# A two-layer hybrid decoder trunk: block products from the fourth inner tile on, weight rests and summed inputs formed by transfers

## The chip, the cores and the metric

The kernel runs on one core of a Trainium2 chip. The metric is the device time of one execution in microseconds (us); the median of several runs is compared. One further execution is taken under the hardware profiler, and all views quoted here are of that one.

The engines are named as the profile names them: PE is the matrix engine (PEld its weight loads), DVE the vector engine, ACT the scalar engine, POOL the GpSimd engine, SP the engine that issues most transfers. Work on one engine runs in the order in which it was laid down when the program was built; engines wait for one another by semaphores.

## The reference

A sequence of 512 tokens of width 1024 passes two layers. The first mixes tokens with a state-space layer (S5), the second with forgetting attention (FoX); behind each stands a gated feed-forward network with a causal convolution of width 3. Every sub-layer's input is normed and modulated.

```python
def modulate(x, g, shift, scale):
    return rmsnorm(x, g) * (1.0 + scale) + shift

def conv_ffn(h, w_up, conv_w, conv_b, w_down):
    up = h @ w_up                        # 1024 -> 2 * 2816
    a, b = jnp.split(up, 2, axis=-1)
    ap = jnp.pad(a, ((0, 0), (CONV_W - 1, 0), (0, 0)))
    a_conv = conv_b
    for i in range(CONV_W):
        a_conv = a_conv + ap[:, i:i + S] * conv_w[i]
    return (jax.nn.silu(a_conv) * b) @ w_down

for i in range(DEPTH):                   # DEPTH = 2
    hn = modulate(h, norm_g[i, 0], *...)
    m = s5_mixer(hn, ...) if i % 2 == 0 else fox_mixer(hn, ...)
    h = h + gate * m
    hn = modulate(h, norm_g[i, 1], *...)
    h = h + gate * conv_ffn(hn, ...)
return rmsnorm(h, final_g)
```

All inputs are float32.

## The kernel before

**Products in parts.** A float32 operand is kept as two parts, hi (the value rounded to the matrix engine's float32r type) and lo (the rest, value minus hi). A product of two operands is three matmuls into one accumulator: hi with hi, hi with lo, lo with hi (`mms`, L304). Weights come in by a transfer issued on SP into a buffer "raw" (`raw`, L192; three buffers). `put_parts` makes hi on ACT (L287) and lo on DVE, `lo = raw - hi` (L288). hi and lo of weights lie in five buffers each (w_hi and w_lo), used in turn; a buffer comes free when PE has used it.

**A network.** Each network's inner width of 2816 is 22 inner tiles f of 128. An inner tile has two weight tiles of 1024 x 128: 2f for the convolved branch, 2f+1 for the other. `gated` takes their products: convolution in three steps (ACT L618, DVE L620 twice), SiLU on ACT (L623), the product with the other branch on DVE (L627), and the split of the result into ghi and glo (ACT L287, DVE L288). The inner tiles come in four groups of 6, 5, 6 and 5. While a group is made, `down` multiplies the group before it with w_down (eight products in all per group, dealt out over the group's tiles) and adds them to the residual stream h (DVE L378). In the first network `tick` adds two rows of later modulation parameters per tile from f=6 on (DVE L256).

**Whole tiles and block tiles.** A whole tile (`up`) is 96 matmuls of 128 x 256: two weight tiles, 8 slices of the input width, 2 halves of the tokens, 3 parts. A block tile (`quarters`) takes the two weight tiles as a 2 x 2 matrix of blocks a11, a12, a21, a22 (each four slices deep) and the input as 2 x 2 blocks (first and second half of its width, first and second half of the tokens), and forms the result from seven block products in place of eight: 7 x 4 x 3 = 84 matmuls (L566). For that it sums blocks of weights on DVE (L537: s1 to s4, in the buffers "sums", four instructions 512 wide), splits them (two more splits 1024 wide, one 512 wide for a22), copies four partial results on ACT (L573), and adds partial results on DVE (L537, four instructions 256 wide, out of the accumulators).

Its input forms t1 to t4 are made once per network by `forms_x`: first the normed input's two parts are added, x = a_hi + a_lo, into two buffers of 128 x 4 x 512 (DVE L500, four instructions), then four forms are subtracted (DVE L506) and split (ACT L287, DVE L288). `forms_x` is a generator; the network's loop takes three steps of it in each whole tile from f=1 on, and what is left before the first block tile.

`WHOLE_TILES` (L49) names the whole tiles of each network: f = 0, 1, 2, 3, 4, 8, 11, 14, 17, 20 in the first, f = 0 to 3 in the second. So there are 12 and 18 block tiles. f=0 and f=1 begin as one group of three weight tiles (the head), first half of the tokens first, so that the second half of the input can still be normed meanwhile (DVE L445 and L449, ACT L448).

**Order.** The framework's scheduler lays every engine's instructions in one order when the program is built, from the order in which they are written, from their dependences, and from its estimate of when each becomes ready. So a change in one place can move instructions on several engines. In the S5 layer the last step of `s5_inputs` (a product, then transposes by PE, L979, L988 and L990, copied out by ACT L989) stands among the first products of the next stage; its accumulators are taken from the pool "aux" (four), while large products mostly use the pool "mmp" (four).

Of the kernel before, what the change touches and what calls it, by code (L numbers as in the profile page):

```python
# [8 lines left out]
F32 = mybir.dt.float32  # L9
# [3 lines left out]
ALU = mybir.AluOpType  # L13
# [32 lines left out]
ROWS_FROM = 0  # L46
GROUPS = (6, 5, 6, 5)
TAIL = 4
WHOLE_TILES = (0, 1, 2, 3, 4, 8, 11, 14, 17, 20), (0, 1, 2, 3)  # L49
SUMS = (0,) * 6 + (2,) * 16  # L50
FIRST = (("c", (KT,)), ("s5_prm", (3, G // 2)))
REST = (
# [11 lines left out]
class Trunk:  # L64
# [6 lines left out]
    def __init__(self, tc, io, ctx):  # L71
        self.tc, self.nc, self.io, self.ctx = tc, tc.nc, io, ctx
        nc = self.nc
        pool = lambda name, bufs, **k: ctx.enter_context(tc.tile_pool(name=name, bufs=bufs, **k))
        self.const = pool("const", 1)
        self.act = pool("act", 1)
        self.wpool = pool("wpool", 3)
        self.tmp = pool("tmp", 2)
        self.small = pool("small", 2)
        self.dram = pool("dram", 1, space=DRAM)  # L80
        self.mm = pool("mm", 4, space=PSUM)
        self.aux = pool("aux", 4, space=PSUM)
        self.bg, self.late = [], ()
        self.acc = None
        self.pending = None
        self.rests, self.odd = 0, False
# [185 lines left out]
    def split(self, src, shape, pool=None, bufs=WB, off=None):  # L272

        if off:
            more = TAIL_ROOM - math.prod(shape[1:])
            hi, lo = (self.wide(pool, n, {"bufs": bufs}, F32R, more, off[n], shape) for n in ("w_hi", "w_lo"))
        elif pool:
            hi, lo = (pool.tile(shape, F32R, name=n, bufs=bufs) for n in ("w_hi", "w_lo"))
        else:
            hi = self.wpool.tile(shape, F32R, name="w_hi", bufs=WB)  # L280
            lo = self.rest(shape, odd=self.odd)
        self.put_parts(hi, lo, self.raw(shape, src))
        return hi, lo

    def put_parts(self, hi, lo, src):
        nc = self.nc
        nc.scalar.activation(hi, src, AF.Copy)  # L287
        self.late = (nc.vector.tensor_tensor(lo, src, hi.bitcast(F32), ALU.subtract).ins,)  # L288

    def weights(self, w, nk, *pool):  # L290
# [199 lines left out]
    def forms_x(self, pool, x, b):  # L490
# [1 line left out]
        nc = self.nc  # L492
        H, N = KT // 2, S // 2
        t1, t2 = HALVES
        normed = self.last_lo.ins
        for j, t in enumerate(b):
            for c in HALVES:
                k = slice(j * H, (j + 1) * H)
                with self.tc.issue_after(normed):
                    nc.vector.tensor_tensor(t[:, :, c], x[0][:, k, c].bitcast(F32), x[1][:, k, c].bitcast(F32), ALU.add)  # L500
                yield
        self.tx = {}

        def form(n, u, v):
# [21 lines left out]
        form(3, b[1][:, :, t2], b[0][:, :, t2])  # L526
        yield

    def quarters(self, pool, l, f, x, finish):

        nc = self.nc
        H, N = KT // 2, S // 2
# [4 lines left out]
        sub = lambda o, u, v, op=ALU.subtract: nc.vector.tensor_tensor(o, u, v, op)  # L537
        w = {}

        def parts(src, names, where=None):  # L540
            shape = [P, len(names) * H, P]
            hi, lo = where or (self.wpool.tile(shape, F32R, name="w_hi", bufs=WB), self.rest(shape, odd=True))
            self.put_parts(hi, lo, src)
            for j, n in enumerate(names):
                w[n] = hi[:, j * H:(j + 1) * H], lo[:, j * H:(j + 1) * H]

        parts(a, ("a11", "a12"))
        sub(c[:, 0], a21, a22, ALU.add)
        sub(c[:, 1], c[:, 0], a11)
        parts(c.rearrange("p n k m -> p (n k) m"), ("s1", "s2"))  # L550
# [43 lines left out]
        sub(ob[:, t1], p1, c4)  # L594
        finish(2 * f + 1, ob, slice(0, S))

    def ffn(self, i, l, x, nxt, whole, sums=()):

        nc, tc = self.nc, self.tc
        with tc.tile_pool(name=f"ffn{l}", bufs=1, reuse_waits="tile") as pool:  # L600
# [49 lines left out]
            for q, n in enumerate(GROUPS):  # L650
                for j, f in enumerate(range(first[q], first[q + 1])):
# [14 lines left out]
                    else:  # L666
                        while todo:
                            if next(todo[0], True):
                                todo.pop()
                        self.quarters(pool, l, f, x, gated)  # L670
                    if q:
                        down(q - 1, range(j * KT // n, (j + 1) * KT // n))
                    self.tick(sums[f] if f < len(sums) else 0)
            self.done()
            down(last, range(KT), tail=TAIL, tail_pool=(pool, 4, TAIL_OFF))
# [122 lines left out]
class S5(Trunk):  # L798
# [163 lines left out]
    def s5_inputs(self, m):  # L962
# [10 lines left out]
        dd = pool.tile([P, P], F32, name="dd", bufs=1)  # L973
        nc.sync.dma_start(dd, self.io["s5_dd"][m])
        part = lambda k, r: x[:, k, r].rearrange("p c j -> p (c j)")
        pk = self.aux.tile([P, 2, P], F32, name="aux")
        for r in range(2):
            for k in range(H4):
                nc.tensor.matmul(  # L979
# [298 lines left out]
class Kernel(S5):  # L1278
# [32 lines left out]
    def fox_values(self, pool, x):  # L1311
# [9 lines left out]
        def load(q):  # L1321
# [3 lines left out]
            out = []  # L1325
            for a in range(0, KT, step):
                j = min(step, KT - a)
                hi, lo = self.split(src[:, a:a + j, :], [P, j, n])
                out += [(hi[:, i, :], lo[:, i, :]) for i in range(j)]
            return out  # L1330

# [172 lines left out]
def build(tc, io, out, stop=None):  # L1504
    with ExitStack() as ctx:
# [97 lines left out]
```

## Time and profile before

| | us |
|---|---|
| median of 3 runs | 1193.88 |
| the runs | 1202.24, 1192.06, 1193.88 |
| the profiled execution | 1197.65 |
| its span, first to last instruction | 1195.9 |
| PE busy | 1174.1 |
| DVE busy | 988.7 |
| ACT busy | 592.4 |
| POOL busy | 62.6 |

The span runs from the first to the last instruction of the profiled execution; 1.75 us of its time lie outside. In the timeline views each row gives the start, the length, the engine, the source line, the operation, the tile written and the tiles read, shapes, and how many instructions were merged, with the idle time before it and what ended that in brackets. The views by stretch give the start and end of a stretch, its length, and for PE, PEld, DVE, ACT and POOL the busy time and the count of instructions, then the granted clock of PE, the busy share of the transfer engines and GB/s. Where a stretch is asked for one source line, only the engines that run it are listed. Lengths of instructions that follow each other overlap a little, so what one costs in a row of them is read from start to start.

### The profile page before, as it was taken

Reading aid. Unit: us, or ns where it says so; the run is one execution under the profiler, and the core shown is the slowest. Engines: PE = TensorE matmul, PEld = TensorE weight load, DVE = VectorE, ACT = ScalarE, POOL = GpSimd, SP = SyncE. Lnnn points to the kernel's source line nnn. Section 1 sums busy time; section 2 is a strip of 40 time slices with the busy share of each in tenths; the row PEclk is TensorE's granted clock in tenths of the full one; section 3 lists DMA queues with packets and bytes.
Section 4 is the critical chain, followed back from the end, with each engine's and each line's share of the span. In section 5 each row is a group of like instructions: output and inputs, shape, how many; then the busy total and the mean of one; then the engine's idle time right before and its main releaser. Section 6 shows DMA issues by size and latency. Waiting matters only on the chain.

```text
span 1195.9 us, 21116 instructions
## 1 busy us (share of the span) xinstructions
PE 1174.1 (98%) x8243; PEld 1026.5 (86%) x8243; DVE 988.7 (83%) x1824; ACT 592.4 (50%) x1069; POOL 62.6 (5%) x114
## 2 busy tenths in 40 slices
PE   7999999999999999999999999999999999999997
PEld 2455687899999999999899788878999999999987
DVE  8899977889888888887776788866899888888855
ACT  2554525346544454453453566554466555555543
POOL 1000000000000000000000443330000000000000
PEclk9999989999999999999999999999999999999999
DMA  9687758822264455554514655523123342343331
GB/s 359 226 256 251 230 167 303 295 92 89 87 204 131 159 174 170 185 184 139 194 36 138 209 185 166 200 76 97 47 75 96 124 124 86 111 124 95 104 88 72
DMA packets 73234, 183.83 MB, mean 154 GB/s; under 512 B 23231, under 2 KB 25503, under 8 KB 72111
## 3 DMA queue, kind: packets, MB, share of 16 engines
q1 hardware_dynamic: 72847, 181.96, 46.6%
q8 instruction: 65, 1.06, 0.4%
q10 hardware_dynamic: 288, 0.52, 0.1%
q14 instruction: 34, 0.28, 0.1%
HBM read 175.53 MB, written 6.92 MB: 153 GB/s over the span
## 4 chain that ended last, share of the span: by engine, by line
PE 86%; DVE 7%; DMA 3%; ACT 2%; issue 1%; POOL 0%; SPq 0%; DVEq 0%; ACTq 0%; POOLq 0%
PE mmp L304 42%; PE mmp L566 15%; PE aux L566 6%; PE mmp L1167 4%; PE mmp L1344 3%; PE mmp L1197 2%; DVE w_lo L288 2%; PE aux L1490 2%; PE aux L1473 1%; PE aux L1061 1%; PE aux L1053 1%; PE mmp L221 1%; PE aux L1443 1%; ACT w_hi L287 1%; DMA raw<-in_w_down 1%
## 5 line engine op out<-in xcount | busy, mean ns | idle before, releaser
L287 ACT ACTIVATE w_hi<-raw 128x1024 fp32r<-128x1024 f32 (+4 forms) x197 | 176.0, 900 | 146.9 <-PE mmp L304 75.5
L288 DVE TENSOR_TENSOR w_lo<-raw,w_hi 128x1024 fp32r<-128x1024 f32 (+4 forms) x197 | 203.4, 1036 | 29.7 <-ACT w_hi L287 25.2
L304 PE MATMUL mmp<-a_hi,w_hi 128*128 128x256 f32 (+1 forms) x600 | 185.9, 311 | 0.0
L304 PE MATMUL mmp<-a_hi,w_lo 128*128 128x256 f32 (+1 forms) x600 | 182.8, 306 | 0.0
L304 PE MATMUL mmp<-a_lo,w_hi 128*128 128x256 f32 (+1 forms) x600 | 182.7, 305 | 0.0
L304 PE MATMUL mmp<-ghi,w_hi 128*128 128x512 f32 (+1 forms) x392 | 143.9, 367 | 0.0
L304 PE MATMUL mmp<-glo,w_hi 128*128 128x512 f32 (+1 forms) x392 | 143.9, 367 | 0.0
L304 PE MATMUL mmp<-ghi,w_lo 128*128 128x512 f32 (+1 forms) x392 | 143.6, 366 | 0.0
L304 PEld LDWEIGHTS mmp<-a_hi,w_hi 128*128 128x128 f32 x600 | 112.4, 188 | 7.6 <-issue 2.6
L304 PEld LDWEIGHTS mmp<-a_hi,w_lo 128*128 128x128 f32 x600 | 112.5, 188 | 6.4
L304 PEld LDWEIGHTS mmp<-a_lo,w_hi 128*128 128x128 f32 x600 | 112.6, 188 | 4.8
L287 ACT ACTIVATE w_hi<-sums 128x1024 fp32r<-128x1024 f32 x68 | 71.6, 1060 | 65.9 <-DVE sums L537 27.4
L566 PE MATMUL mmp<-w_hi 128*128 128x256 f32 x360 | 99.6, 277 | 0.0
L566 PE MATMUL mmp<-w_hi,w_lo 128*128 128x256 f32 x360 | 99.5, 276 | 0.0
L566 PE MATMUL mmp<-w_lo,w_hi 128*128 128x256 f32 x360 | 99.4, 276 | 0.0
L288 DVE TENSOR_TENSOR w_lo<-sums,w_hi 128x1024 fp32r<-128x1024 f32 x68 | 82.4, 1220 | 7.6 <-ACT w_hi L287 6.5
L256 DVE CUSTOM_DVE_ANT_0 ada_raw<-ada_raw,ada_c,rest 128x1024 f32<-128x1024 f32 x64 | 83.7, 1326 | 5.1 <-DMA ada_raw<-in_ada_rows 5.1
L304 PEld LDWEIGHTS mmp<-ghi,w_lo 128*128 128x128 f32 x392 | 73.6, 188 | 12.3
L304 PEld LDWEIGHTS mmp<-ghi,w_hi 128*128 128x128 f32 x392 | 73.6, 188 | 11.2
L304 PEld LDWEIGHTS mmp<-glo,w_hi 128*128 128x128 f32 x392 | 73.6, 188 | 11.1
L378 DVE SCALAR_TENSOR_TENSOR h<-mmp,par,h 128x512 f32<-128x512 f32 (+1 forms) x98 | 62.9, 649 | 23.4 <-PE mmp L304 23.3
L566 PEld LDWEIGHTS mmp<-w_hi 128*128 128x128 f32 x360 | 67.6, 188 | 0.1
(317 smaller groups left out, 2833.0 us busy)
## 6 DMA issues: line engine op xcount, KB each, us to landing
raw<-in_w_up SPq DMA_DIRECT2D x88, 512.0 KB, 3.4
ada_raw<-in_ada_rows SPq DMA_DIRECT2D x64, 512.0 KB, 4.2
raw<-in_ada_w SPq DMA_DIRECT2D x32, 512.0 KB, 5.5
raw<-in_w_down SPq DMA_DIRECT2D x32, 384.0 KB, 3.2
raw<-in_w_down SPq DMA_DIRECT2D x32, 320.0 KB, 3.1
nf<-nfd SPq DMA_DIRECT2D x8, 1152.0 KB, 5.7
raw<-in_fox_qk SPq DMA_DIRECT2D x16, 512.0 KB, 3.2
h<-in_x SPq DMA_DIRECT2D x8, 512.0 KB, 5.5
```

What stands on the lines that cost most here:

```text
L221: self.last_mm = nc.tensor.matmul(ps[32 * qq:32 * qq + 32, :], self.sc32[:, k, :], w[:, q * S:(q + 1) * S], start=(step is steps[0]), stop ...
L256: nc.vector.tensor_tensor_reduce(w, w, self.crow, 1.0, self.ada_b[:, i, m:m + 1], ALU.mult, ALU.add, self.par[i][:, m:m + 1])
L287: nc.scalar.activation(hi, src, AF.Copy)
L288: self.late = (nc.vector.tensor_tensor(lo, src, hi.bitcast(F32), ALU.subtract).ins,)
L304: self.last_mm = self.nc.tensor.matmul(o, wt, xt[:, cols], start=(k == 0 and n == 0), stop=(k == nk - 1 and n == 2),)
L378: self.nc.vector.scalar_tensor_tensor(h, v, self.par[i][:, 16 + m:17 + m], h, op0=ALU.mult, op1=ALU.add,).ins,
L566: self.last_mm = nc.tensor.matmul(o, wt[:, k], xt[:, k], start=(first and k == 0 and n == 0), stop=(k == H - 1 and n == 2), skip_group_che ...
L1053: nc.tensor.matmul(yp[g2][:, k, :], t[:, 2 * k + g2], u[:, g, :], start=(k == 0), stop=False, skip_group_check=True,)
L1167: nc.tensor.matmul(ps, w[m][:, k, :], x[:, k], start=(k == 0), stop=(k == KT - 1))
L1197: nc.tensor.matmul(gps[m], wt, xt[:, k], start=(k == 0 and part == 0 and xt is yhi), stop=(k == KT - 1 and part == 1))
L1344: self.last_mm = nc.tensor.matmul(ps[q, b][:, :n], xt[:, k, tb], wt, start=(k == 0 and i == 0), stop=(k == KT - 1 and i == 2),)
L1490: nc.tensor.matmul(pv[:, c * P:], self.v[:, hp, k, r].rearrange("p t d -> p (t d)"), pp[:, r, c + 3 * k:NB + 3 * k, :].rearrange("p b t -> ...
```

## The change

Four edits. The whole tiles are now f = 0, 1, 2 in both networks, so each has 19 block tiles. The adds of the input's parts become twelve transfers per network issued by POOL: four copies of a_hi (512 KB) and eight transfers of a_lo (256 KB) that add to what lies in the buffer. In the first network, lo of each block tile's first weight tile and of the down weights of all but the last group is made as minus hi on ACT, to which a transfer issued by POOL adds the weights once more from DRAM; the same holds for two loads of the attention's value weights. And the last step of `s5_inputs` takes its first accumulator from the other pool.

```diff
-WHOLE_TILES = (0, 1, 2, 3, 4, 8, 11, 14, 17, 20), (0, 1, 2, 3)
+WHOLE_TILES = (0, 1, 2), (0, 1, 2)
...
-        self.put_parts(hi, lo, self.raw(shape, src))
+        self.put_parts(hi, lo, self.raw(shape, src), src if self.by_dma else None)
         return hi, lo
 
-    def put_parts(self, hi, lo, src):
+    def put_parts(self, hi, lo, src, again=None):
         nc = self.nc
         nc.scalar.activation(hi, src, AF.Copy)
+        if again is not None:
+            nc.scalar.activation(lo, hi.bitcast(F32), AF.Copy, scale=-1.0)
+            nc.gpsimd.dma_start(lo, again, accum_op=ALU.add)
+            return
         self.late = (nc.vector.tensor_tensor(lo, src, hi.bitcast(F32), ALU.subtract).ins,)
...
     def forms_x(self, pool, x, b):
...
-        normed = self.last_lo.ins
-        for j, t in enumerate(b):
+        for n, step in enumerate((4, 2)):
             for c in HALVES:
-                k = slice(j * H, (j + 1) * H)
-                with self.tc.issue_after(normed):
-                    nc.vector.tensor_tensor(t[:, :, c], x[0][:, k, c].bitcast(F32), x[1][:, k, c].bitcast(F32), ALU.add)
-                yield
+                for j, t in enumerate(b):
+                    for a in range(0, H, step):
+                        k = slice(j * H + a, j * H + a + step)
+                        nc.gpsimd.dma_start(
+                            t[:, a:a + step, c], x[n][:, k, c].bitcast(F32), accum_op=ALU.add if n else ALU.bypass
+                        )
...
-    def quarters(self, pool, l, f, x, finish):
+    def quarters(self, pool, l, f, x, finish, by_dma):
...
-        parts(a, ("a11", "a12"))
+        parts(a, ("a11", "a12"), again=self.io["w_up"][l][2 * f] if by_dma else None)
...
-                        self.quarters(pool, l, f, x, gated)
+                        self.quarters(pool, l, f, x, gated, by_dma)
                     if q:
+                        self.by_dma = by_dma
                         down(q - 1, range(j * KT // n, (j + 1) * KT // n))
+                        self.by_dma = False
...
-        pk = self.aux.tile([P, 2, P], F32, name="aux")
+        pk = self.mm.tile([P, S], F32, name="mmp")[:, :2 * P] if m == KT - 1 else self.aux.tile([P, 2 * P], F32, name="aux")
+        pk = pk.rearrange("p (n c) -> p n c", n=2)
...
+                self.by_dma = q == 1
                 hi, lo = self.split(src[:, a:a + j, :], [P, j, n])
+                self.by_dma = False
...
-        x = k.ffn(1, 0, x, k.norm_mod(2), WHOLE_TILES[0], SUMS)
+        x = k.ffn(1, 0, x, k.norm_mod(2), WHOLE_TILES[0], SUMS, True)
```

In the changed kernel L287 and L292 are the two halves of a split, L289 and L290 the pass that makes minus hi and the transfer that adds, L504 the transfers of the input's sum, L511 the forms, L542 the sums, L571 the block products, L625 the convolution's steps and L632 the gate product.

More of the change, by code (lines that the diff above doesn't have):

```diff
@@ L85, in __init__ @@
         self.pending = None
-        self.rests, self.odd = 0, False
+        self.rests, self.odd, self.by_dma = 0, False, False
         self.ones = self.const.tile([P, P], F32, name="ones")
@@ L538, in quarters, with parts @@
         w = {}
-        def parts(src, names, where=None):
+        def parts(src, names, where=None, again=None):
             shape = [P, len(names) * H, P]
             hi, lo = where or (self.wpool.tile(shape, F32R, name="w_hi", bufs=WB), self.rest(shape, odd=True))
-            self.put_parts(hi, lo, src)
+            self.put_parts(hi, lo, src, again)
             for j, n in enumerate(names):
                 w[n] = hi[:, j * H:(j + 1) * H], lo[:, j * H:(j + 1) * H]
-        parts(a, ("a11", "a12"))
+        parts(a, ("a11", "a12"), again=self.io["w_up"][l][2 * f] if by_dma else None)
         sub(c[:, 0], a21, a22, ALU.add)
@@ L595, in quarters, with ffn @@
         finish(2 * f + 1, ob, slice(0, S))
-    def ffn(self, i, l, x, nxt, whole, sums=()):
+    def ffn(self, i, l, x, nxt, whole, sums=(), by_dma=False):
         nc, tc = self.nc, self.tc
```

## The prediction

> **What bounds the kernel now.** I read the page first (busy time, chain of waits), then busy time by stage, then the timelines of VectorE (DVE) and ScalarE (ACT) around the first block tile of each network.
>
> ```profile
> PE 1174.1 (98%) x8243; PEld 1026.5 (86%) x8243; DVE 988.7 (83%) x1824; ACT 592.4 (50%) x1069; POOL 62.6 (5%) x114
> PE 86%; DVE 7%; DMA 3%; ACT 2%; issue 1%; POOL 0%; SPq 0%; DVEq 0%; ACTq 0%; POOLq 0%
> ```
>
> TensorE (PE) is busy nearly always and holds 86% of the chain that ended last. The next view gives busy time in stretches: a whole tile (f=8), a block tile (f=5), two down products and a middle stretch of the first network, then the first three block tiles of the second.
>
> ```profile
> core 0: us, PE busy (x) PEld busy (x) DVE busy (x) ACT busy (x) POOL busy (x), PEclk, DMA share, GB/s
> 310.34:319.89 9.55, 9.55 (x87) 9.55 (x86) 8.03 (x13) 6.62 (x11) 0.00 (x0) 1.00 0.28 88
> 351.20:362.11 10.91, 10.91 (x97) 10.91 (x96) 7.29 (x10) 3.40 (x4) 0.00 (x0) 1.00 0.54 182
> 450.00:480.00 30.00, 30.00 (x236) 28.80 (x235) 26.22 (x41) 15.03 (x23) 0.00 (x0) 1.00 0.56 177
> 890.93:919.82 28.89, 28.89 (x255) 28.79 (x253) 28.53 (x44) 18.12 (x31) 0.00 (x0) 1.00 0.35 117
> ```
>
> A whole tile holds PE for 10.91 us, a block tile for 9.55, or 0.1137 per matmul, 1.36 per product of twelve. PE never idles there. But in the second network DVE is busy 28.53 of 28.89 us: PE and DVE are level, and three tiles take 0.24 more than 3 x 9.55. So matmuls taken away pay only while DVE's splits, sums and forms keep ahead.
>
> **The change, part by part.** *Matmuls.* Seven tiles of the first network and one of the second become block tiles: 8 x 1.36 = **-10.9**, the whole of what can be won in the networks.
>
> *The forms come early.* The first block tile is now f=3. In the first network it starts two whole tiles before 310.34, at 288.5, in the second one before 890.93, at 880.0. DVE's prices are read from start to start in its timeline, first network:
>
> ```profile
> 270.19 4.62 DVE L500 TENSOR_TENSOR x<-a_hi,a_lo 128x1024 f32<-128x1024 f32 x4
> 274.73 2.71 DVE L620 SCALAR_TENSOR_TENSOR conv<-mmp,conv_wb,conv 128x511 f32<-128x511 f32 x4
> 277.36 2.35 DVE L288 TENSOR_TENSOR w_lo<-raw,w_hi 128x1024 fp32r<-128x1024 f32 x2
> 279.63 1.27 DVE L627 TENSOR_TENSOR conv<-conv,mmp 128x512 f32<-128x512 f32 x2
> 280.82 1.22 DVE L288 TENSOR_TENSOR w_lo<-raw,w_hi 128x1024 fp32r<-128x1024 f32 x1
> 281.96 1.28 DVE L288 TENSOR_TENSOR glo<-conv,ghi 128x512 fp32r<-128x512 f32 x2
> 283.17 1.22 DVE L506 TENSOR_TENSOR sums<-x 128x1024 f32<-128x1024 f32 x1
> 284.30 0.74 DVE L620 SCALAR_TENSOR_TENSOR conv<-mmp,conv_wb,conv 128x511 f32<-128x511 f32 x1
> ...
> 299.48 1.28 DVE L537 TENSOR_TENSOR sums<-raw 128x512 f32<-128x512 f32 x2
> 300.69 0.68 DVE L627 TENSOR_TENSOR conv<-conv,mmp 128x512 f32<-128x512 f32 x1
> ...
> 331.08 0.42 DVE L537 TENSOR_TENSOR nm_t<-mmp,nm_h 128x256 f32<-128x256 f32 x1
> 331.42 0.74 DVE L620 SCALAR_TENSOR_TENSOR conv<-nm_t,conv_wb,conv 128x510 f32<-128x510 f32 x1
> ```
>
> Four conv steps take 2.63, a wide split 1.14, a form 1.13, a gate product, a gate rest or a weight sum 0.60, one conv step 0.66 (a quarter of the four), an output sum 0.34.
>
> The first place is DVE's order at the entry of the first network (x_2514 and x_2515 are the two summed halves of the input, sums the forms). Before:
>
> ```order
> L500 TENSOR_TENSOR x_2514<-a_hi,a_lo 128x4x256 x2
> L500 TENSOR_TENSOR x_2515<-a_hi,a_lo 128x4x256 x2
> L620 SCALAR_TENSOR_TENSOR conv<-mmp,conv_wb,conv 128x511 x2
> L620 SCALAR_TENSOR_TENSOR conv<-mmp,conv_wb,conv 128x510 x2
> L288 TENSOR_TENSOR w_lo<-raw,w_hi 128x1024 x2
> ```
>
> and now:
>
> ```order
> L625 SCALAR_TENSOR_TENSOR conv<-mmp,conv_wb,conv 128x511 x2
> L625 SCALAR_TENSOR_TENSOR conv<-mmp,conv_wb,conv 128x510 x2
> L511 TENSOR_TENSOR sums<-x_2514 128x1024
> L511 TENSOR_TENSOR sums<-x_2515,sums 128x1024
> L632 TENSOR_TENSOR conv<-conv,mmp 128x512 x2
> ```
>
> The adds are gone, the forms stand right behind the conv steps. The conv steps wait for the head's products, so DVE gains no time ahead of them: 274.73 stays. From there to the split of s1, which f=3 needs, now stand 4 conv steps (2.63), 4 forms (4.52), their 4 splits (4.54), 3 gate products and 3 rests (3.6), 2 conv steps (1.32), 4 weight sums (2.42), an output sum (0.34) and the split (1.14): 20.5, so 295.2. PE puts three products ahead of s1, to 292.6: **+2.5**. If DVE or PE shift a little, 0 to 4.
>
> Second network:
>
> ```profile
> 861.71 4.63 DVE L500 TENSOR_TENSOR x<-a_hi,a_lo 128x1024 f32<-128x1024 f32 x4
> 866.25 2.72 DVE L620 SCALAR_TENSOR_TENSOR conv<-mmp,conv_wb,conv 128x511 f32<-128x511 f32 x4
> ```
>
> Here one raw split more stands between and its output sum does not (21.3): s1 at 887.5 against 884.1, a stall of 3.4. The next s1 comes 9.1 of DVE later, at 896.6; PE wants it two products into f=4, which begins four products after 887.5: 895.7, stall 0.9. f=5 stalls 0, f=6 (10.3 of DVE) 0.3. Less the 0.24 of before: **+4.4**, 2 to 6.
>
> *The sums by transfer.* The second place is POOL's queue. Before:
>
> ```order
> L136 MEMSET elo_gap 128x8
> L136 MEMSET x_gap 128x16
> L136 MEMSET ehi_gap 128x16
> L136 MEMSET v_gap 128x32
> L1306 MEMSET lf_one 16x512
> ```
>
> and now (two copies, four accumulations, for each half of the tokens):
>
> ```order
> L136 MEMSET ehi_gap 128x16
> L504 DMA x_2514<-a_hi 128x4x256
> L504 DMA x_2515<-a_hi 128x4x256
> L504 DMA x_2514<-a_lo 128x2x256 x2
> L504 DMA x_2515<-a_lo 128x2x256 x2
> L504 DMA x_2514<-a_hi 128x4x256
> L504 DMA x_2515<-a_hi 128x4x256
> L504 DMA x_2514<-a_lo 128x2x256 x2
> L504 DMA x_2515<-a_lo 128x2x256 x2
> L290 DMA w_lo<-in_w_up 128x1024 x4
> L290 DMA w_lo<-in_w_down 128x768
> ```
>
> Twelve transfers stand ahead of every weight rest. An accumulation waits for its copy to land; behind it POOL's next waits, and DVE's forms wait for the last. The trace has no transfer issued by POOL and none that adds; nearest rows, and ACT's last write of the normed input:
>
> ```profile
> raw<-in_w_up SPq DMA_DIRECT2D x88, 512.0 KB, 3.4
> nf<-nfd SPq DMA_DIRECT2D x8, 1152.0 KB, 5.7
> u<-s_ud SPq DMA_DIRECT2D x8, 256.0 KB, 4.5
> ```
>
> ```profile
> 268.84 0.91 ACT L448 ACTIVATE a_hi<-nm_h,par 128x256 fp32r<-128x256 f32 x2 [1.05 <-DVE nm_h L445]
> ...
> 284.04 1.06 ACT L287 ACTIVATE w_hi<-raw 128x1024 fp32r<-128x1024 f32 x1
> 285.00 1.04 ACT L287 ACTIVATE w_hi<-sums 128x1024 fp32r<-128x1024 f32 x1
> ```
>
> 269.75 + 3.4 + 4.5 = 277.7; DVE wants the second form at 278.5. With 2.3 more for the four issues on the way (my choice) it lands at 280.0: **+1.5** in the first network; both hops doubled, 285.5, +7. In the second the order leaves more room: 0.
>
> *Weight rests by transfer.* 43 splits of 1.14 or less leave DVE in the first network (19 a, 24 down), two in the values of attention; ACT gains as many passes of 0.96 and POOL as many accumulations. The third place is ACT at f=3 and f=4. Before, at its first block tiles (w_hi<-raw 128x1024 is the next tile's a):
>
> ```order
> L287 ACTIVATE w_hi<-raw 128x1024
> L623 ACTIVATE conv<-conv 128x512
> L573 ACTIVATE nm_h<-mmp 128x256 x2
> L287 ACTIVATE ghi<-conv 128x512
> L573 ACTIVATE nm_h<-mmp 128x256
> ```
>
> and now:
>
> ```order
> L287 ACTIVATE ghi<-conv 128x512
> L287 ACTIVATE w_hi<-sums 128x1024 x2
> L287 ACTIVATE w_hi<-raw 128x1024
> L287 ACTIVATE w_hi<-raw 128x512
> L289 ACTIVATE w_lo<-w_hi 128x1024
> ```
>
> All loads of weights in the first network's block stretch, issue (ns) and landing:
>
> ```profile
> L192 SPq DMA_DIRECT2D raw<-in_w_up x30: 327/328/504, 312.3 to 529.1; - x30
> ...
> DMA to landing us min/median/max: 2.8/3.8/6.5
> ```
>
> f=4's a now stands behind f=3's sums, whose last is made at 294.1 + 1.5. Four ACT passes (3 x 0.96 + 0.6) end at 299.3; the accumulation lands about 6 later (5.7, the row that moves about two operands' bytes, and 0.33 of issue), at 305.3. PE is at f=4 four products after s1 (296.7 + 5.46 + 0.2 = 302.4): **+2.9**. Bounds: a plain load and an issue, 3.7, 0.6; twice the 6.5 of the slowest load, 13, 9.9.
>
> [...]
>
> Later tiles have more lead, and DVE has room (two down products; a modulation row):
>
> ```profile
> 343.03:351.20 8.17, 8.17 (x36) 6.76 (x37) 1.00 0.37 112
> ```
>
> ```profile
> L256 DVE CUSTOM_DVE_ANT_0 ada_raw<-ada_raw,ada_c,rest 128x1024 f32<-128x1024 f32 x32 | 39.8, 1279 | 0.0
> ```
>
> ```profile
> 415.96 1.06 ACT L287 ACTIVATE w_hi<-raw 128x1024 fp32r<-128x1024 f32 x1 [1.76 <-PE mmp L304]
> ```
>
> ```profile
> 428.96:438.51 9.55, 9.55 (x84) 9.51 (x83) 1.00 0.90 275
> ```
>
> ACT takes f=10's a at 415.96; PE begins f=10 at 428.96. Two passes leave 11.1 for POOL and the transfer. DVE per tile keeps two splits (2.28), a22's (0.6), four sums (2.42), four outputs (1.36), conv steps, product and rest (2.52), two modulation rows (2.56) and one and a half residuals, each as wide as a conv step (1.0): 12.7, beside PE's 9.55 + 1.5 x 4.09 = 15.7. So **0**, covered by PE's down products and that lead; without the lead each us comes back in every tile.
>
> *S5.* The last tile's product moves to the other PSUM pool:
>
> ```profile
> 141.23 0.33 PE L990 MATMUL aux<-rest,ktt 128*128 128x128 f32 x1 [0.28 <-DVE ktt L983]
> 142.96 0.66 PE L988 MATMUL aux<-rest,x 128*128 128x128 f32 x4 [1.41 <-ACT w L989]
> ```
>
> The order now has all eight transposes ahead of that turn: of 1.7 idle I take **-1.0** (0 to -1.7).
>
> Sum: -10.9 + 2.5 + 4.4 + 1.5 + 2.9 - 1.0 = **-0.6**. The profiled execution took 1197.65 (span 1195.9), 3.77 above the median of 1193.88 of three runs (1192.06 to 1202.24); so 1197.05, or **1193.3** as a median.
>
> **Rivals.** *No stall at the entry.* If DVE and transfers come in time, only -10.9 - 1.0 is left: 1182. For it: PE has no idle in any block tile now; against: DVE's 28.53 of 28.89. 15%.
>
> *Rests later than their lead* (slower). Past 11.1 us from ACT's pass to landing, each us is paid by each of the 16 block tiles from f=6 on, and by f=4. At 13: 2 x 16 + 7 = +39, 1232. For it: the transfer engines are at a share of 0.56 already, and about 1 MB a tile comes on top. Against: plain loads land in 3.4, a third of the lead. [...] 17%.
>
> *The summed input late in both networks.* Hops of twice the rows' length: +5.5 and some 3 in the second: 1202. 13%.
>
> **Numbers.** Forecast 55%, with its own range of 1187 to 1200. The range goes from 1183, most of the first rival, to 1212, leaving out most of the second. Within 1% (about what this kernel's measurement tells from no change) is 1182 to 1206: faster 0.05, same 0.73, slower 0.22.
>
> **What would show it.** Block tiles of 9.55 from f=6 on with PE unbroken; PE idle 3 to 5 us at f=3 of each network, released by VectorE's w_lo, and 1 to 5 at f=4 of the first by a transfer; L290 landing in 4 to 8. Wrong, if PE waits for w_lo transfers in most tiles, or the head of the second network is no longer than before.

## The result: slower, by two gaps of which the forecast had seen almost nothing

The changed kernel took 1249.13 us as a median of four runs (1247.49 to 1256.67), against 1192.97 (1191.68 to 1202.24) for the kernel before: a ratio of 1.047, with a 95% interval of 1.043 to 1.0509. I had forecast 1193.3.

The page of the changed kernel: busy time, PE and its granted clock in 40 slices, and the chain that ended last.

```profile
PE 1175.7 (94%) x8147; PEld 1024.9 (82%) x8147; DVE 978.9 (79%) x1851; ACT 652.5 (52%) x1162; POOL 125.6 (10%) x183
...
PE   7999999993899999999999999999939999999997
...
PEclk9999999995899999999999999999959999999999
...
PE 66%; issue 14%; DVE 8%; DMA 6%; ACT 3%; POOL 2%; DVEq 0%; POOLq 0%; SPq 0%; ACTq 0%
```

96 matmuls are gone (8243 before, 8147 now) and PE is still busy for as long (1174.1 before, 1175.7 now). PE's slices are full but for two, one at each network's entry, where the granted clock falls to a half as well. In the chain, "issue" (time in which an engine waited for nothing that the profile shows) has risen from 1% to 14%, but that is not the gaps: 105.8 of these some 174 us stand between 339 and 466 us, where PE is busy for 126.87 of 127.00 us and the chain runs through POOL. So the loss is read from the stretches and not from this share. The next view goes through the first gap in stretches.

```profile
core 0: us, PE busy (x) PEld busy (x) DVE busy (x) ACT busy (x) POOL busy (x), PEclk, DMA share, GB/s
276.00:282.00 6.00, 6.00 (x55) 6.00 (x55) 0.00 (x0) 0.00 (x0) 1.04 (x2) 1.00 0.32 126
282.00:286.00 4.00, 0.35 (x4) 0.15 (x2) 0.00 (x0) 0.00 (x0) 1.23 (x1) 0.87 0.34 97
286.00:290.00 4.00, 0.00 (x0) 0.00 (x0) 0.00 (x0) 0.00 (x0) 1.21 (x1) 0.50 0.43 67
290.00:305.00 15.00, 3.00 (x12) 2.71 (x13) 6.83 (x8) 3.93 (x5) 3.29 (x3) 0.50 0.49 81
...
316.00:318.00 2.00, 1.96 (x10) 1.67 (x9) 2.00 (x3) 2.00 (x4) 0.00 (x0) 0.50 0.85 262
318.00:320.00 2.00, 2.00 (x14) 2.00 (x14) 2.00 (x5) 0.98 (x2) 0.84 (x1) 0.72 0.00 0
320.00:324.00 4.00, 3.50 (x31) 3.30 (x29) 2.73 (x6) 3.64 (x6) 0.00 (x0) 1.00 0.86 162
```

From 276 to 290 neither DVE nor ACT does anything at all. What DVE waits for stands in its timeline (start, duration; in brackets the idle time ahead and what ended it), and then PE's first matmul of f=3, with two a little later:

```profile
268.75 2.71 DVE L625 SCALAR_TENSOR_TENSOR conv<-mmp,conv_wb,conv 128x511 f32<-128x511 f32 x4
291.41 1.23 DVE L511 TENSOR_TENSOR sums<-x 128x1024 f32<-128x1024 f32 x1 [19.94 <-DMA x<-a_lo]
299.39 1.23 DVE L511 TENSOR_TENSOR sums<-x,sums 128x1024 f32<-128x1024 f32 x1 [6.76 <-DMA x<-a_lo]
300.54 1.28 DVE L632 TENSOR_TENSOR conv<-conv,mmp 128x512 f32<-128x512 f32 x2
```

```profile
301.27 0.58 PE L571 MATMUL mmp<-a_hi,w_hi 128*128 128x256 f32 x1 [18.93 <-DVE conv L632]
...
303.18 0.41 PE L571 MATMUL mmp<-a_hi,w_hi 128*128 128x256 f32 x1
303.39 0.41 PE L571 MATMUL mmp<-a_lo,w_hi 128*128 128x256 f32 x1
```

The forms wait for the input's sum, and the gate products of f=0 and f=1 (L632) stand behind the first two forms in DVE's order, so PE stops for want of room for its results (PSUM, the buffers of its accumulators). POOL's timeline shows why the sum is late. These are the twelve transfers of one network and the first weight rest:

```profile
249.59 0.94 POOL L504 DMA_DIRECT2D x<-a_hi  x1 [84.81 <-ACT a_hi L452]
253.37 0.79 POOL L504 DMA_DIRECT2D x<-a_hi  x1 [2.84 <-DMA x<-a_hi]
259.36 1.22 POOL L504 DMA_DIRECT2D x<-a_lo  x1 [5.20 <-DVE a_lo L453]
...
283.68 1.23 POOL L504 DMA_DIRECT2D x<-a_lo  x1 [2.80 <-issue]
287.65 1.21 POOL L504 DMA_DIRECT2D x<-a_lo  x1 [2.75 <-issue]
291.60 1.18 POOL L504 DMA_DIRECT2D x<-a_lo  x1 [2.73 <-issue]
295.55 1.19 POOL L504 DMA_DIRECT2D x<-a_lo  x1 [2.78 <-issue]
296.28 1.38 POOL L290 DMA_DIRECT2D w_lo<-in_w_up  x1
```

One accumulation starts 3.95 to 3.97 us behind the other (287.65 less 283.68, 291.60 less 287.65, 295.55 less 291.60). The operands have long been there, yet the "idle" of 2.75 ends with "issue". Twelve take 46 us, 249.6 to 295.6. The second network repeats it:

```profile
869.26 0.84 POOL L504 DMA_DIRECT2D x<-a_hi  x1 [37.31 <-PE aux L399]
...
916.34 1.20 POOL L504 DMA_DIRECT2D x<-a_lo  x1 [2.73 <-DVE conv L632]
```

Between the gaps the block tiles run as forecast, and the weight rests land somewhat later than that. A later block tile (f=8) and the landing of the weight rests, L290:

```profile
375.29:384.84 9.55, 9.55 (x85) 9.54 (x84) 9.27 (x14) 5.16 (x7) 1.30 (x2) 1.00 0.94 227
```

```profile
DMA to landing us min/median/max: 4.4/6.7/10.1
```

For the comparisons below I cut each profiled execution at the start of ScalarE's last pass over the normed input of each network. The first stretch runs from that pass in the first network to that in the second (the first network and attention), the second stretch from there to the end. What stands ahead of the first cut is left out, for a reason given under the S5 run. Each stretch is of one execution: before and s5_only, whose networks are the same, differ by 0.3 and 1.1. Each ratio is to the kernel before as it was measured beside that run (medians 1192.29 to 1193.28 for the experiments).

| kernel | first stretch, us | second stretch, us | median, us | ratio to before (95%) |
|---|---|---|---|---|
| before | 591.5 | 335.1 | 1192.97 | |
| after | 619.3 | 363.3 | 1249.13 | 1.047 (1.043 to 1.0509) |
| adds_back | 591.5 | 341.8 | 1200.77 | 1.0067 (1.0047 to 1.0087) |
| rests_back | 645.9 | 363.8 | 1276.45 | 1.0704 (1.0625 to 1.0783) |
| forms_only | 617.3 | 363.0 | 1244.88 | 1.0426 (1.0397 to 1.0455) |
| tiles_only | 622.9 | 343.6 | 1231.47 | 1.032 (1.0292 to 1.0349) |
| small_steps | 604.3 | 347.2 | 1220.34 | 1.0212 (1.0174 to 1.0251) |
| plain_lo | 596.2 | 342.3 | 1209.78 | 1.0125 (1.0102 to 1.0148) |
| merged | 597.1 | 345.0 | 1208.2 | 1.012 (1.0091 to 1.015) |
| second_rests | 594.0 | 341.1 | 1208.59 | 1.0124 (1.0097 to 1.0152) |
| late_entry | 586.2 | 336.9 | 1191.17 | 0.9985 (0.9967 to 1.0002) |
| late_entry2 | 587.8 | 335.2 | 1189.82 | 0.9971 (0.9957 to 0.9986) |
| s5_only | 591.8 | 336.2 | 1191.95 | 0.9992 (0.9973 to 1.0011) |

After against before, that is +27.8 in the first stretch and +28.2 in the second, 56.0 of the 56.2 between the medians. The medians of adds_back and small_steps each count one execution far out, of 2348.89 and of 4150.28 us; without it they are 1199.89 and 1220.33, and the ratios leave it out.

### The profile page after: what moved, and what is told of

Its sections match the earlier page's. It is cut to its first block, busy times and chain, and to the rows that moved or that the text cites. A ratio compares the mean times of both kernels' runs of the same rounds, so it can differ in the third digit from the quotient of the medians.

```text
span 1246.2 us, 21201 instructions
## 1 busy us (share of the span) xinstructions
PE 1175.7 (94%) x8147; PEld 1024.9 (82%) x8147; DVE 978.9 (79%) x1851; ACT 652.5 (52%) x1162; POOL 125.6 (10%) x183
## 4 chain that ended last, share of the span: by engine, by line
PE 66%; issue 14%; DVE 8%; DMA 6%; ACT 3%; POOL 2%; DVEq 0%; POOLq 0%; SPq 0%; ACTq 0%
PE mmp L308 27%; PE mmp L571 13%; PE aux L571 5%; PE mmp L1354 3%; PE mmp L1175 3%; DVE w_lo L292 2%; PE mmp L1205 2%; PE aux L1500 2%; PE aux L1483 1%; DMA w_lo<-in_w_up 1%; POOL x L504 1%; DMA raw<-in_w_down 1%; PE aux L1069 1%; PE aux L1061 1%; POOL w_lo L290 1%
## 5 line engine op out<-in xcount | busy, mean ns | idle before, releaser
L287 ACT ACTIVATE w_hi<-raw 128x1024 fp32r<-128x1024 f32 (+4 forms) x197 | 172.1, 881 | 125.8 <-PE mmp L308 56.8
L292 DVE TENSOR_TENSOR w_lo<-raw,w_hi 128x1024 fp32r<-128x1024 f32 (+4 forms) x152 | 151.8, 1000 | 35.2 <-ACT w_hi L287 31.3
L287 ACT ACTIVATE w_hi<-sums 128x1024 fp32r<-128x1024 f32 x84 | 88.1, 1058 | 92.2 <-DVE sums L511 53.8
L571 PE MATMUL mmp<-w_hi 128*128 128x256 f32 x456 | 128.7, 282 | 7.5 <-ACT w_hi L287 6.2
L571 PE MATMUL mmp<-w_lo,w_hi 128*128 128x256 f32 x456 | 127.6, 280 | 0.0
L571 PE MATMUL mmp<-w_hi,w_lo 128*128 128x256 f32 x456 | 127.1, 281 | 0.1
L571 PE MATMUL mmp<-a_hi,w_hi 128*128 128x256 f32 x304 | 85.8, 283 | 32.6 <-DVE conv L632 32.5
L308 PE MATMUL mmp<-a_hi,w_hi 128*128 128x256 f32 (+1 forms) x344 | 115.4, 337 | 0.0
L308 PE MATMUL mmp<-a_lo,w_hi 128*128 128x256 f32 (+1 forms) x344 | 112.1, 327 | 0.3
L308 PE MATMUL mmp<-a_hi,w_lo 128*128 128x256 f32 (+1 forms) x344 | 112.1, 327 | 0.0
L292 DVE TENSOR_TENSOR w_lo<-sums,w_hi 128x1024 fp32r<-128x1024 f32 x84 | 101.4, 1218 | 3.7 <-ACT w_hi L287 2.5
L571 PEld LDWEIGHTS mmp<-w_hi 128*128 128x128 f32 x456 | 87.5, 192 | 9.0 <-ACT w_hi L287 7.1
L571 PE MATMUL mmp<-a_hi,w_lo 128*128 128x256 f32 x304 | 86.1, 283 | 1.6 <-DMA w_lo<-in_w_up 1.5
L571 PEld LDWEIGHTS mmp<-w_hi,w_lo 128*128 128x128 f32 x456 | 86.8, 191 | 0.8 <-DVE w_lo L292 0.7
L571 PEld LDWEIGHTS mmp<-w_lo,w_hi 128*128 128x128 f32 x456 | 87.4, 192 | 0.0
L571 PEld LDWEIGHTS mmp<-a_hi,w_hi 128*128 128x128 f32 x304 | 58.1, 191 | 34.4 <-DVE conv L632 32.9
L571 PE MATMUL mmp<-a_lo,w_hi 128*128 128x256 f32 x304 | 85.5, 281 | 0.0
```

The lines of the kernel that those rows point to most:

```text
L308: self.last_mm = self.nc.tensor.matmul(o, wt, xt[:, cols], start=(k == 0 and n == 0), stop=(k == nk - 1 and n == 2),)
L571: self.last_mm = nc.tensor.matmul(o, wt[:, k], xt[:, k], start=(first and k == 0 and n == 0), stop=(k == H - 1 and n == 2), skip_group_che ...
```

## The experiments

### The sum back on VectorE, and the rests back on VectorE

Two runs undo one half of the transfers each. First the adds:

```diff
 # forms_x, of the changed kernel (adds_back); the loops and their order, changed with it, are left out
-nc.gpsimd.dma_start(t[:, a:a + step, c], x[n][:, k, c].bitcast(F32), accum_op=ALU.add if n else ALU.bypass)
+nc.vector.tensor_tensor(t[:, :, c], x[0][:, k, c].bitcast(F32), x[1][:, k, c].bitcast(F32), ALU.add)
```

> The changed kernel with the normed input summed by VectorE again (four adds per network) and nothing else undone. Theory (the twelve transfers in POOL's queue stand one behind the other, some 3.9 us each, 46 us in all, and hold the forms back in both networks): the forms come when VectorE is free, PE's gaps of 19 and 14 us at the first block tile go, and so does the clock of 0.5 behind them. 1197.65 profiled before, less 10.9 for matmuls, less 6.5 for the S5 stage as the trace after shows it, plus the 9.8 us of entry stalls that I predicted without transfers of the sum, is 1190 profiled, a median near 1186 (1178 to 1194). Rival (block products from the fourth tile on are too early for VectorE whatever sums the input): the gaps stay, with 4.5 us more work on VectorE ahead of them, and the time stays above 1230.

Measured: 1200.77. PE's waits in the two networks (what PE waited for, us in total, times, longest), first and second:

```profile
PE mmp L570 <- ACT w_hi L287: 2.6, 1, 2.6
...
PE mmp L570 <- ACT nm_h L577: 1.4, 2, 1.2
PE mmp L570 <- DMA w_lo<-in_w_up: 1.2, 3, 0.5
PE mmp L570 <- DVE w_lo L292: 0.5, 1, 0.5
```

```profile
PE mmp L570 <- DVE w_lo L292: 2.4, 2, 1.9
PE mmp L570 <- ACT w_hi L287: 1.4, 1, 1.4
```

Both gaps are gone, and with them 27.8 and 21.5 us: 49 of the 56. The theory stands for them, and my figure for what is left does not: not 1186 but 1200.8, past the 1194 at the end of my range. Nor is the clock of 0.5 quite gone: it is at 0.86 on average over 286 to 298. The first network is level with before although it has seven tiles less to carry in full (9.5 us of matmuls), the second is 6.7 slower.

```diff
 # the program and fox load, of the changed kernel (rests_back)
-x = k.ffn(1, 0, x, k.norm_mod(2), WHOLE_TILES[0], SUMS, True)
+x = k.ffn(1, 0, x, k.norm_mod(2), WHOLE_TILES[0], SUMS)
-self.by_dma = q == 1
```

> The changed kernel with the weight rests of the first network and of the attention values on VectorE again; the input is still summed by transfers. Theory (the twelve transfers alone): the gap in the first network stays where it is, 1240 to 1256. Rival (the rests that wait in POOL's queue behind the twelve transfers, or land late in every tile, cost a good part): at least 15 us come back, under 1235.

Measured: 1276.45, above both ranges. The rival is refuted, and the sign is the opposite: the weight rests by transfer earn 26.6 us of the first stretch (645.9 against 619.3). The gap stays without them, so it is not they that cause it.

### The tables alone, and the transfers of the sum alone

```diff
 # of the kernel before (tiles_only)
-WHOLE_TILES = (0, 1, 2, 3, 4, 8, 11, 14, 17, 20), (0, 1, 2, 3)
+WHOLE_TILES = (0, 1, 2), (0, 1, 2)
```

> The kernel before with only the table of whole tiles changed (block products from the fourth tile on in both networks, everything else on VectorE as before). If PE is the bound and VectorE keeps up in the first network without the transfers, -10.9 for the matmuls and some 7 us of entry stalls: 1187 to 1192. If VectorE cannot carry 43 more splits than the change leaves it beside block products, it falls behind in nearly every tile of the first network (its work per tile is about 15.5 us against PE's 15.7 on average, so a miss of 1 us a tile is 18 us): 1200 to 1215.

Measured: 1231.47, worse than either reading. In the first network PE waits for rests and high parts all along:

```profile
PE mmp L566 <- DVE w_lo L288: 9.4, 10, 2.1
PE mmp L566 <- ACT w_hi L287: 7.2, 7, 2.8
```

Without the rests by transfer, VectorE cannot carry block products in every tile: +31.4 in the first stretch. With them (adds_back) it is 0. That is what they are worth here, and all that they buy is that the seven block tiles cost nothing.

```diff
 # forms_x, of the kernel before (forms_only); the loops are left out
-nc.vector.tensor_tensor(t[:, :, c], x[0][:, k, c].bitcast(F32), x[1][:, k, c].bitcast(F32), ALU.add)
+nc.gpsimd.dma_start(t[:, a:a + step, c], x[n][:, k, c].bitcast(F32), accum_op=ALU.add if n else ALU.bypass)
```

> The kernel before with only the normed input's sum moved to the twelve transfers per network; tables and rests as before. Theory (a chain of 46 us whatever stands around it): the last transfer lands some 36 us after the normed input, the forms and their splits follow, and the first block tiles, which start 41 and 30 us after it, wait for them 5 to 15 and 15 to 25 us: 1212 to 1235. Rival (the chain is that long only beside the rests by transfer, or the two later tiles hide it): 1190 to 1198.

Measured: 1244.88, more than I had expected, and nearly the whole loss. A later first block tile hides little of the chain (25.8 and 27.9 us are lost in the two stretches), and PE's waits and DVE's timeline say why:

```profile
PE mmp L304 <- DVE conv L628: 14.6, 1, 14.6
PE mmp L567 <- ACT nm_h L574: 4.5, 1, 4.5
```

```profile
293.00 1.23 DVE L507 TENSOR_TENSOR sums<-x 128x1024 f32<-128x1024 f32 x1 [22.51 <-DMA x<-a_lo]
...
295.28 1.28 DVE L628 TENSOR_TENSOR conv<-conv,mmp 128x512 f32<-128x512 f32 x2
```

L304 is the whole tiles' product. PE's long wait is not at f=5, the first tile that uses the forms (there it waits 4.5 us, for a copy by ACT); it stops in the whole tiles, because the gate products of f=0 and f=1 that free its PSUM stand behind the first of the waiting forms on DVE. A run with these products ahead of the forms would show how much of the loss is this order; it was not made.

### What the 3.9 us are

Three runs change the transfers and nothing else. In the first they are cut in half, in the second the eight accumulations become plain copies, in the third both halves of the tokens go in one. The second leaves out the addition, so its output is not the kernel's; its timeline is what it is for.

```diff
 # forms_x, of the changed kernel (small_steps)
-for n, step in enumerate((4, 2)):
+for n, step in enumerate((2, 1)):
```

> The changed kernel with the twelve transfers of each network cut into twenty-four of half the size, same bytes and same rows of 1 KB. Three readings of the 3.9 us between one issue and the next: a fixed price of each issue on POOL gives 24 x 3.9 = 94 us from the first to the last, 47 us more in each network, above 1320; the rate at which the transfers move or POOL writes descriptors gives the same 46 us and the same time, 1240 to 1256; a queue that has room for only one transfer of this size at a time, so that each waits until the one ahead has landed (3.7 us), lets two or three half-size ones overlap: 20 to 32 us from first to last, and a time of 1205 to 1232.

Measured: 1220.34. POOL's timeline, the end of the chain in the first network:

```profile
270.43 0.92 POOL L504 DMA_DIRECT2D x<-a_lo  x1 [1.84 <-DMA x<-a_hi]
271.06 1.03 POOL L504 DMA_DIRECT2D x<-a_hi  x1
271.78 1.22 POOL L504 DMA_DIRECT2D x<-a_lo  x1
273.36 0.85 POOL L504 DMA_DIRECT2D x<-a_lo  x1 [0.37 <-issue]
```

Twenty-four transfers take less time than twelve: 250.4 to about 279, 29 us against 46, for the same bytes in the same rows, as the third reading has it. So it is neither a price of the issue nor the bytes nor the rows that POOL has to write: the halves above start 0.63 to 1.58 us one behind the other, where wholes that add stood 3.95 apart.

```diff
 # forms_x, of the changed kernel (plain_lo)
-accum_op=ALU.add if n else ALU.bypass
+accum_op=ALU.bypass
```

> The changed kernel with the eight accumulations of each network's input sum made plain copies of the same rows, to the same places (left out: the addition, so the forms are made of the low parts alone). Theory (a transfer waits for room in POOL's queue, and one that adds takes twice the room because it reads two operands): the 256-row copies go two or three at a time, one issue 1.0 to 2.5 us behind the other in place of 3.96, the chain falls from 46 us to 25 to 35, and the time to 1210 to 1235. Rival (POOL needs a fixed time for a row or an issue, adding or not): 3.9 us between issues and 1240 to 1256 as before.

Measured: 1209.78, a chain of 24 us (249.8 to 273.6), both just past the good end of what I had written.

```profile
249.77 0.91 POOL L504 DMA_DIRECT2D x<-a_hi  x1 [84.83 <-ACT a_hi L452]
253.53 0.77 POOL L504 DMA_DIRECT2D x<-a_hi  x1 [2.84 <-DMA x<-a_hi]
254.28 0.71 POOL L504 DMA_DIRECT2D x<-a_lo  x1
259.70 2.14 POOL L504 DMA_DIRECT2D x<-a_lo  x3 [4.71 <-DVE nm_h L449]
```

A copy of 512 rows still starts 3.76 behind another of 512, but one of 256 starts 0.75 behind it, and three of 256 go within 2.14. Adding was what kept transfers of 256 rows apart. In the changed kernel transfers of 256 rows that add start 3.95 to 3.97 us one behind the other (above) and land 3.6 to 3.7 us after their issue (283.68 to 295.55), so each starts some 0.3 us behind the landing of the one ahead; a weight rest of 128 rows, which adds too, starts 0.73 behind the last of them (295.55 and 296.28). That agrees with a wait for the transfer ahead. The theory's reason, room in a queue of which one that adds takes twice as much, was not shown: no trace has the queue's fill, nor what an adding transfer reads.

```diff
 # forms_x, of the changed kernel (merged)
-for n, step in enumerate((4, 2)): ...
+for n in range(2):
+    for j, t in enumerate(b):
+        nc.gpsimd.dma_start(t, x[n][:, j * H:(j + 1) * H].bitcast(F32), accum_op=ALU.add if n else ALU.bypass)
```

> The changed kernel with the input summed by four transfers per network in place of twelve: both token halves at once, 1 MB each in rows of 8 KB, two copies and two accumulations. If a transfer fills the queue by its rows (512 or 256 rows of 1 KB there, 128 of 8 KB here), the four are issued without waiting for each other, and the sum lands some 10 to 14 us after VectorE's last low part, near 275 to 279 us, against VectorE's wish for it near 272: the gaps of 19 and 14 us go and 2 to 7 stay, 1193 to 1208. If it is the bytes, 1 MB takes four times a 256 KB transfer's 3.9 us, some 46 us in all again, and the time is 1240 to 1256.

Measured: 1208.2. Of the four transfers of 1 MB in 128 long rows, whose first starts at 260.92, none has a wait that ends with "issue":

```profile
263.55 0.56 POOL L501 DMA_DIRECT2D x<-a_hi  x1 [1.92 <-ACT a_hi L452]
266.24 0.89 POOL L501 DMA_DIRECT2D x<-a_lo  x1 [2.13 <-DMA x<-a_hi]
269.09 0.86 POOL L501 DMA_DIRECT2D x<-a_lo  x1 [1.97 <-DVE w_lo L292]
271.06 0.89 POOL L290 DMA_DIRECT2D w_lo<-in_w_up  x1 [1.10 <-ACT w_lo L289]
```

The forms start at 275.40, and the second at 281.39, where the twelve transfers let them start at 291.41 and 299.39. The chain is cured, at the slow end of what I had written, and the kernel is still 7 us slower than with VectorE's four adds. Here the two hops through the transfer engines cost more than 4.6 us of adds that stand on the spot.

### Where the entry lies

Three runs keep VectorE's adds and move the first block tile, or take more from VectorE.

```diff
 # WHOLE_TILES with VectorE's adds: late_entry, then late_entry2
-WHOLE_TILES = (0, 1, 2), (0, 1, 2)
+WHOLE_TILES = (0, 1, 2, 3, 4), (0, 1, 2, 3)
+WHOLE_TILES = (0, 1, 2, 3), (0, 1, 2, 3)
```

> The changed kernel with the input summed by VectorE, and with the first block tile where it was (f=5 in the first network, f=4 in the second); the weight rests of the first network stay with the transfers, and five of its tiles (8, 11, 14, 17, 20) stay block tiles. Theory (what the kernel with VectorE's adds lost against my sum, 14 us, is VectorE's work at an entry that comes too early): the entry costs nothing again, five tiles save 6.8 us, and some 3 go to waits in the later tiles: 1185 to 1191. Rival (the loss sits in the later tiles, in rests that land late): 1192 or more.

> As the run with the first block tile where it was before the change, but with the fifth tile of the first network a block tile too (its first block tile is f=4): 1.36 us of matmuls less. If the entry is VectorE's work against the time that whole tiles give it, one tile less of 10.9 us leaves 0 to 4 us of waits there: 1189 to 1195. If VectorE had slack at f=5 that f=4 does not use up, 1189 to 1190.

Measured: 1191.17, at the edge of the theory's range and not to be told from before, and 1189.82, which both readings allow and which beats both kernels: 0.9971, with an interval of 0.9957 to 0.9986. In the first of the two PE waits 0.5 us in the first network's tiles:

```profile
PE mmp L570 <- ACT nm_h L577: 0.5, 1, 0.5
```

Its first stretch is 5.3 below before, of 6.8 us of matmuls taken out. Against it, adds_back has two more block tiles there (2.7 us of matmuls) and is 5.3 longer, so the early entry costs 8.0; in the second network one tile (1.4) and 4.9, so 6.3.

```diff
 # of adds_back (second_rests)
-k.ffn(3, 1, x, k.norm_out(out), WHOLE_TILES[1])
+k.ffn(3, 1, x, k.norm_out(out), WHOLE_TILES[1], by_dma=True)
```

> The changed kernel with VectorE's adds, and with the second network's weight rests by transfer too. Theory (the waits left at the entry of the second network, 7.6 us, are VectorE's queue): each split of weights that leaves VectorE between the forms and the sums of f=3 and f=4 gives 1.14 back, two or three of them 2 to 3.5 us: 1196 to 1199. Rival (they are set by other work, or the rests land too late at f=3): 1200 or more.

Measured: 1208.59. The second stretch is 341.1 against 341.8: the wait only changes its releaser.

```profile
PE mmp L570 <- ACT w_hi L287: 2.6, 1, 2.6
PE mmp L570 <- DMA w_lo<-in_w_up: 1.9, 2, 1.1
```

The theory that single splits set the second network's entry falls; and the 7.6 us of waits that it started from are 4.1 in the trace of adds_back (2.4, 1.4 and 0.3). Why the median is another 8 above adds_back, the second stretch does not show. In the profiled execution most of it stands ahead of the first network, which starts 7.5 us later; that is the next subject. All four executions of second_rests show a lower mean granted clock (0.981 to 0.989) than eight of the nine usual ones of adds_back (0.991 to 0.994; the ninth 0.986). Whether the edit brings that about stays open.

### The S5 stage

```diff
 # of the kernel before (s5_only)
-pk = self.aux.tile([P, 2, P], F32, name="aux")
+pk = self.mm.tile([P, S], F32, name="mmp")[:, :2 * P] if m == KT - 1 else self.aux.tile([P, 2 * P], F32, name="aux")
+pk = pk.rearrange("p (n c) -> p n c", n=2)
```

> The kernel before with only the last product of the S5 stage moved to the other PSUM pool. The profile after starts its first network 5.7 us earlier than the profile before, whose granted clock fell to 0.5 in that stage. Theory A (that fall belongs to the one profiled execution, not to the kernel): 0 to -1 us, 1191 to 1193. Theory B (the move itself keeps PE busy enough for the full clock): -4 to -7 us, 1185 to 1188.

Measured: 1191.95, a ratio of 0.9992 (0.9973 to 1.0011): theory A, and of the -1.0 in my sum nothing can be told. The stretch from 145 to 155 us, of the kernel before, then of tiles_only, whose S5 stage has the same code:

```profile
145.00:155.00 10.00, 10.00 (x77) 9.24 (x76) 8.76 (x14) 6.23 (x15) 0.35 (x4) 0.50 0.42 123
```

```profile
145.00:155.00 10.00, 10.00 (x105) 8.75 (x104) 10.00 (x17) 7.92 (x19) 0.34 (x4) 1.00 0.44 134
```

The same code ran at half the clock in one profiled execution and at the full clock in the other. That costs some 4 to 6 us (worked out under the hardware below), more than the 3.77 between the 1197.65 of the execution I argued from and the median of 1193.88, and it is why the table starts behind it.

## Why the prediction was wrong, point by point

*The sum by transfer: the step that failed.* "With 2.3 more for the four issues on the way (my choice) it lands at 280.0: +1.5 in the first network; both hops doubled, 285.5, +7. In the second the order leaves more room: 0." What the forms waited for landed until 299.4, and the step cost 27.8 and 21.5. I had quoted POOL's queue with its twelve transfers in a row, and then priced the two hops of a single pair, at the latency of transfers that another queue had issued, with 0.57 for each issue. Doubling a hop did not bound the unknown, which was how fast POOL's queue takes the next one: 3.95 us, seven times my price, and twelve stand in line. The bound from the other side would have been twelve transfers in series at the quoted landings of 3.4 and 4.5: 4 x 3.4 + 8 x 4.5 = 50 us, and the chain took 46.

*Who is behind the waiting instruction.* I had written that the forms wait for the last transfer, and showed the gate products right behind them in DVE's order. That PE's whole tiles would stop for them I had not drawn; forms_only shows it, where no block tile is near.

*The summed input late in both networks (13%).* The right mechanism at a fifth of its size: 7 and 3 us for hops twice as long, where 27.8 and 21.5 were measured. Its price repeats the step above.

*Matmuls, -10.9.* Right: a block tile holds PE for 9.55 us (375.29 to 384.84), and late_entry, with 60 matmuls fewer than s5_only, keeps PE busy for 1161.9 us against 1169.0, 7.1 less where 6.8 were due; the granted clock is 0.997 in both. (The 1174.1 of before is no measure for this: it holds an S5 stage at half the clock.)

*Early entry, +2.5 and +2.9 in the first network, +4.4 in the second.* Right in kind and short in size. With VectorE's adds, which my sum had taken away, the entry costs 8.0 and 6.3 against my 5.4 and 4.4. PE's waits at the entry come to only 4.2 and 4.1 of that. A term that I had put at nothing is the clock, which in adds_back stood at 0.86 on average over 286 to 298 and at 0.92 over 870 to 892, by estimate 12 x 0.14 = 1.7 and 22 x 0.08 = 1.8 us. (In the +2.9, four passes from 295.6 end at 299.1 and not at 299.3.) The four adds are 4.6 of VectorE's time in each network; what they cost and what the early tile costs cannot be parted by these runs, since no transfer of the sum came in time to replace the adds without a wait of its own. What they do show is that two tiles later the entry is as good as free: late_entry waits 0.5 us there.

*Rests later than their lead (17%), and 0 for the later tiles.* The rival is refuted. The rests land in 4.4 to 10.1 us, none above the 11.1 I had worked out, and PE's waits for them come to 1.5 us. The nineteen of 512 KB from w_up took 5.2 to 10.1; their median, 7.5, is above my 6. The sum of VectorE's work per tile, 12.7 beside PE's 15.7, was for the kernel with these transfers; that VectorE falls behind without them I had not worked out, and tiles_only shows it, 31.4 us.

*S5, -1.0.* Not to be told from nothing.

*What would show it.* Block tiles of 9.55 from f=6 on came true, and the landings of L290 nearly (4 to 8 stated). PE's idle time at f=3 was not 3 to 5 us released by w_lo but 18.9, released by a gate product. Neither of my two signs of being wrong came (PE waiting for w_lo transfers in most tiles, a second network with no longer head): both watched other terms than the queue.

## What to carry to other kernels

Price a queue by its rate as well as by a transfer's latency: how many transfers stand ahead of the one that is waited for, and whether the second can start before the first has landed. On POOL's queue 512 rows of 1 KB started 3.76 us behind another 512, and 256 that add 3.95 behind 256 that add, where three copies of 256 went within 2.14; none of the transfers of 1 MB in 128 long rows had a wait that ended with "issue", and weight rests of 128 rows went by at the side at little cost (PE waited 1.5 us for them). And look at what stands behind an instruction that waits: here the products that free PSUM stood behind it, and the tiles that need none of the forms stopped too.

## What the runs showed of the hardware that was not expected

The granted clock made the gap dearer. PE's last product ended at 282.35, the clock was at 0.50 from 285.0 to 319.1, and one matmul followed the other after 0.21 us in that time (303.18, 303.39), against 0.1137 in the block tiles at the full clock. The second gap had two stretches at half clock, of 13.7 us each, and the entry of adds_back one of 3.4. Ahead of the fall, from 281.6 to 285.0, PE was busy for 0.75 us. In the first half of the 34.1 us (to 302.05) it was busy for 0.78 us, in the second for 11.85 of 17.05; only behind that did the full clock come back. Work without a break from 303.0 to 308.0 did not bring it back. What sets the length of such a stretch was not shown. The 8147 matmuls keep PE busy for 1175.7 us here and for 1163.8 in adds_back, with the S5 stage at the full clock in both, so at most some 12 of the 49 us are the clock's.

The same clock fell to a half in the S5 stage in three of the thirteen profiled executions (the kernel before, second_rests and late_entry2: 0.50, 0.50 and 0.53 at 145 to 155), with and without the moved product. In these ScalarE's last passes over the first network's input start at 267.9 to 269.9, in the other ten at 263.6 on average: some 4 to 6 us. PE did not idle in this stretch: it is busy for all of the 10.00 us in each of the three. Why the clock fell there was not shown. A single profiled execution shows that fall as if it were the kernel's. The mean granted clock of every execution is on record: of 53 of the kernel before, measured beside the experiments, four show 0.993 or less, and they took 1197.5 to 1199.9 us, 5 to 7 more than the medians beside them. Where in those executions it fell is not recorded.

POOL's recorded time for an issue (0.8 to 1.2 us) leaves out the wait ahead of it: the 2.75 us stand in the profile as idle time ended by "issue", and the transfer ahead was under way for most of it (3.6 to 3.7 us from issue to landing).
